# Gathered rows ordered behind the products of each step, and other rates of gathering

## The chip, the cores and the metric

The kernel runs on one core of one Trainium2 chip. The metric is the time of one execution on the device in microseconds (us); less is better. The profile comes from one execution, recorded by the hardware profiler. PE is TensorE (PEld its weight loads), DVE is VectorE, ACT is ScalarE, POOL is GpSimd, SP is SyncE.

## The reference, cut to what matters

Two layers of a transformer trunk run on 256 latent and 256 context tokens of width 1024. Each layer is an adaptive norm, four attention branches, a gated merge, and then an expert layer with a residual. The expert layer is the part that matters here:

```
q = x @ w_q                              # 8 heads, two half queries each
s = q . subkeys ; top 16 of 128 on each half
cand = sums of the two top lists ; best 16 of them -> experts (of 16384), g = softmax(best)
u_sel, v_sel = u[experts], v[experts]    # rows of 1024 floats
a = gelu(x . u_sel)                      # one number for each token, head and choice
y = sum over heads and choices of g * a * v_sel
```

So each token picks 8 x 16 = 128 of 16384 experts; each expert is one row of u and one row of v. The first layer runs this for all 512 tokens, the last layer for the 256 latent tokens alone.

## The kernel before, in words

**Two ways to the same expert layer.** In layer 0, 384 of the 512 tokens take the dense way: all 16384 experts are multiplied (128 blocks of 128 experts), and a matrix G of gate weights, zero for experts that are not chosen, masks the result. The other 128 tokens take the gathered way (class Chosen): for each of the 128 choices, one indirect DMA fetches one row of u for each token, and then, once all dots are known, one row of v for each. That is 256 rows (a "row" here is a tile of 128 tokens x 1024 floats). In layer 1 all 256 tokens are dense.

**The dense stages of layer 0**, in the order of `peer` and `experts`:

- `route` finds the experts. At its end `ahead` runs the first 17 u steps (LEAD0).
- The G stage: u steps 17 to 39 (`u_step`), with 48 g steps between them. A `u_step` loads a block of u, splits it into a high part (ACT, L144) and a low part (L145, on POOL or DVE by a share), and makes 24 products on PE (L183), parked through a Gelu (L753). A `g_step` builds one-hot and gate tiles on DVE (L761, L765, L769) for 8 tokens and multiplies them on PE (L777); the result goes to DRAM. All 48 g steps are asked for by u step 34; the last six u steps follow.
- The mixed steps, 88 of them: `v_step(j)` multiplies a parked block by its gates (L793), splits it and a block of v (L144, L145), and makes 18 products (L804); `u_step(j + 40)` follows it.
- The v steps, the last 40, without a u step.

**The gathered way rides along.** After each u step (G stage) or each v step, `gather()` adds a rate to a counter, and `Chosen.step` runs as many times as the counter holds whole rows. GATHERS holds the rate of the G stage and that of the mixed steps; in the v steps the rate is what is left, divided by 37. One step requests rows until five are under way (AHEAD 4, ROWS 5), and uses the oldest: for u a dot product on DVE (L1085), for v a multiply-add on DVE (L1091). A request is one instruction in POOL's queue (L1062):

```
while self.asked <= min(i + AHEAD, 2 * SLOTS - 1):
    n = self.asked
    self.load()
```

`finish` takes what is left, transposes the result (L1103) and adds it to the residual; `v_end` (L819) does the same for the dense tokens, and the statistics of the next norm follow.

**What sets the order of the work.** Each engine takes its instructions in the order of its own queue. The queues are laid out before the run by a planner that simulates a timeline (`schedule_with_timeline_sim=True`): an instruction is put into its queue when, in the plan, its inputs are there and its engine is free. The program's order ranks what is ready at the same time; it doesn't hold anything back. An explicit edge can: with the kind that is used here (NoSync) an instruction is placed only after another one is placed, and the engines get no semaphore for it. The kernel has one use of such edges, `issue_after` in `route`, between instructions of PE.

Of the kernel before, what the change touches and what calls it, by code (L numbers as in the profile page):

```python
# [55 lines left out]
MB = [2, 3]  # L56
SHARE = [0.64, 0.888, 0.75]
PSH = [[1.0, 0.65, 0.6], [1.0, 0.3, 0.3]]
GATHERS = [1.0, 2.15]
SHL = [0.3, 0.181]  # L60
DIRECT = 7
NST = 16
# [6 lines left out]
class K:  # L69
    def __init__(self, tc, a, out):  # L70
        self.tc, self.nc, self.a, self.out = tc, tc.nc, a, out
        self.n_lo = 0.0
        self.fresh = False
        self.gates = []
        self.rows = None
        self.fill = []
        self.share = 0.5
# [646 lines left out]
    def peer(self):  # L724
# [4 lines left out]
        tc, nc, a, l = self.tc, self.nc, self.a, self.l  # L729
# [3 lines left out]
        lead = LEAD[l]  # L733
        with self.pool("pe") as hp, tc.tile_pool(name="gd", bufs=1, space=bass.MemoryType.DRAM) as dp:
# [9 lines left out]
            P, park, grs, vacc, stage = [], {}, {}, {}, {}  # L744
# [3 lines left out]
            def u_step(j):  # L748
                hi, lo = self.weights(a["u"][l, j])
                ps = self.psum("acc")[:, :n]  # L750
                end = self.mm(ps, hi, lo, lambda kt: P[0][:, kt, :n], lambda kt: P[1][:, kt, :n], DT)
                park[j] = hp.tile([128, n], F32, name="park", tag="park", bufs=lead + 1)
                nc.scalar.activation(park[j], ps, AF.Gelu)  # L753
                return end.ins

            def g_step(t0):
# [32 lines left out]
            def v_step(j):  # L789
                w = park.pop(j)  # L790
                g = grs[j // GI][:, :, j % GI, :]
                w3 = w.rearrange("p (b t) -> p b t", t=GB)
                nc.vector.tensor_mul(w3, w3, g)  # L793
                hi, lo = self.weights(a["v"][l, j])
                whi = vp[0].tile([128, n], F32R, name="whi", tag="whi", bufs=WB)
                wlo = vp[0].tile([128, n], F32R, name="wlo", tag="wlo", bufs=WB)
                self.split(whi, wlo, w, self.lo_engine(n / 1024))
                if j == 0:
                    vacc[0] = [[self.psum("big") for _ in range(2)] for _ in range(nt)]
                for x, y, first, end in ((whi, hi, j == 0, False), (wlo, hi, False, False),  # L800
                                         (whi, lo, False, j == 127)):
                    for t in range(nt):
                        for d in range(2):
                            nc.tensor.matmul(vacc[0][t][d], x[:, t * 128:t * 128 + 128],  # L804
                                             y[:, d * 512:d * 512 + 512], start=first, stop=end)

            def v_end():

# [25 lines left out]
            def phase(i, ns):  # L834

                self.share, self.n_lo = PSH[l][i], 0.0
                if self.chosen:
                    r = GATHERS[i] if i < 2 else (2 * SLOTS - self.chosen.at) / (ns - 3)
                    return lambda: self.chosen.steps(r)
                return lambda: None  # L840

            with self.pool("route") as wk:
                own = None
                if self.chosen:
                    own = wk.tile([128, DT, 128], F32, name="own")
                P[:] = self.norm_mod(wk, hp, NB, LAT if self.last else ALL, 1, n, own)
                self.share = SHARE[2]


                def ahead():  # L850
                    self.share, self.n_lo = PSH[l][0], 0.0
                    return [u_step(j) for j in range(LEAD0[l])][-1]

                self.route(wk, n, *P, own, i1T, i2T, gAB, ahead)
            with self.pool("rows") as p:
                if self.chosen:
                    self.chosen.own = p
                self.experts(l, lead, n, gp, vp, u_step, g_step, g_read, v_step, v_end, phase)
# [169 lines left out]
class Chosen:  # L1028
# [3 lines left out]
    def __init__(self, k, pool):  # L1032
        self.k, self.nc, self.pool = k, k.nc, pool
        self.index = pool.tile([128, SLOTS], I32, name="cx")
        self.g = pool.tile([128, SLOTS], F32, name="cg")
        self.dot = pool.tile([128, SLOTS], F32, name="cd")

        self.h = self.y = pool.tile([128, D], F32, name="ch")
        self.at, self.asked, self.ready, self.due, self.rows = 0, 0, 0, 0.0, []

    def tokens(self, own):

        k, nc = self.k, self.nc
        for i in range(2):
            ps = k.psum("big")
            for j in range(4):
                nc.tensor.transpose(ps[:, j * 128:j * 128 + 128], own[:, i * 4 + j, :], k.ident)
            nc.scalar.activation(self.h[:, i * 512:i * 512 + 512], ps, AF.Copy)
# [7 lines left out]
    def load(self):  # L1056
        nc, i = self.nc, self.asked
        if i == 2 * SLOTS or (i < SLOTS and i >= self.ready):
            return
        self.asked += 1  # L1060
        row = self.own.tile([128, D], F32, name="row", tag="row", bufs=ROWS)
        nc.gpsimd.indirect_dma_start(  # L1062
            out=row, out_offset=None,
            in_=self.k.a["u_rows" if i < SLOTS else "v_rows"],
            in_offset=bass.IndirectOffsetOnAxis(ap=self.index[:, i % SLOTS:i % SLOTS + 1], axis=0))
        self.rows.append(row)

    def step(self):

        nc, i = self.nc, self.at  # L1070
# [3 lines that stand above are left out]
            if n == self.asked:  # L1074
                break
        if not self.rows:
            return
        row = self.rows.pop(0)
        self.at += 1
        s = i % SLOTS  # L1080
        if i == SLOTS:
            nc.scalar.activation(self.dot, self.dot, AF.Gelu)
            nc.vector.tensor_mul(self.g, self.g, self.dot)
        if i < SLOTS:
            nc.vector.scalar_tensor_tensor(row, row, 1.0,  # L1085
                                           self.h, op0=OP.mult, op1=OP.mult,
                                           accum_out=self.dot[:, s:s + 1])
        elif s == 0:
            nc.vector.tensor_scalar(self.y, row, self.g[:, 0:1], None, op0=OP.mult)
        else:  # L1090
            nc.vector.scalar_tensor_tensor(self.y, row, self.g[:, s:s + 1], self.y, op0=OP.mult,  # L1091
                                           op1=OP.add)
# [149 lines left out]
```

## Time and profile before

| what | value |
|---|---|
| time, median of 3 runs | 3394.08 us (3390.36 to 3397.08) |
| the profiled execution: its time | 3400.0 us |
| the profiled execution: its span, first to last instruction | 3397.5 us |
| busy: PE | 3112.5 us (92%) |
| busy: DVE | 2371.5 us (70%) |
| busy: POOL | 1496.1 us (44%) |
| busy: ACT | 1366.0 us (40%) |
| granted PE clock, mean | 0.950 |
| bytes read and written in DRAM | 594.99 MB and 42.99 MB |

The span is cut into stretches by the view of stages: there each engine has its busy time, with the number of its instructions in brackets. "Idle before" in a row of the view by lines is the time the engine stood idle just ahead of these instructions, with what ended it. A granted clock of 1.00 stands for 2.4 GHz, 0.50 for 1.2 GHz, and a mean between them for a stretch that had both.

### The profile page before, as it was taken

How to read it: one execution, taken by the hardware profiler on the slowest of the kernel's cores; microseconds unless marked ns; L12 is line 12 of the kernel's file. 1: busy time of each engine (PE TensorE's matmuls, PEld its weight loads, DVE VectorE, ACT ScalarE, POOL GpSimd, SP SyncE). 2: the span in 40 equal slices, each digit the busy share in tenths (PEclk: the TensorE clock that was granted, in tenths of full speed). 3: DMA queues.
4: the chain of work that ended last, by engine and by line, in shares of the span. 5: the costliest groups of instructions: out<-in, count | busy, mean ns of one | idle time of the engine just before them, and what ended most of it. 6: DMA issues, size and time to landing. Idle time of an engine off the chain costs nothing. (4 is left out here: it accounts for less than half of the span.)

```text
span 3397.5 us, 49459 instructions
## 1 busy us (share of the span) xinstructions
PE 3112.5 (92%) x19063; PEld 2731.2 (80%) x19063; DVE 2371.5 (70%) x4092; ACT 1366.0 (40%) x2166; POOL 1496.1 (44%) x814
## 2 busy tenths in 40 slices
PE   7999999888776798999999998999987889999998
PEld 5867777888666587888899887788987888999987
DVE  5465453799999898989944434445689997666655
ACT  4444443323332233333333333345543454444454
POOL 1211322236656688888844332234435563232221
PEclk9998999899788899999999998899988999999999
DMA  6331333124888988998844333443433569666664
GB/s 245 103 99 50 106 118 110 57 86 149 319 304 304 353 296 299 325 319 296 281 154 143 125 130 116 153 137 106 148 131 120 187 217 308 213 210 212 191 193 136
DMA packets 251292, 641.20 MB, mean 189 GB/s; under 512 B 20017, under 2 KB 107697, under 8 KB 245937
## 3 DMA queue, kind: packets, MB, share of 16 engines
q1 hardware_dynamic: 208432, 461.88, 42.1%
q0 software_dynamic: 36864, 134.23, 11.2%
q10 hardware_dynamic: 5760, 41.95, 3.3%
q8 instruction: 149, 2.44, 0.3%
q14 instruction: 87, 0.70, 0.1%
HBM read 594.99 MB, written 42.99 MB: 188 GB/s over the span
## 5 line engine op out<-in xcount | busy, mean ns | idle before, releaser
L145 POOL TENSOR_TENSOR w_lo<-raw,w_hi 128x1024 fp32r<-128x1024 f32 x387 | 974.8, 2521 | 1336.1 <-ACT w_hi L144 831.2
L144 ACT ACTIVATE w_hi<-raw 128x1024 fp32r<-128x1024 f32 x664 | 702.8, 1060 | 1190.9 <-PE ps_acc L183 437.5
L183 PE MATMUL ps_acc<-hhi,w_hi 128*128 128x256 f32 (+2 forms) x3136 | 997.6, 335 | 56.6 <-ACT w_hi L144 21.0
L183 PE MATMUL ps_acc<-hlo,w_hi 128*128 128x256 f32 (+2 forms) x3136 | 972.4, 328 | 0.3 <-DVE hlo L355 0.3
L183 PEld LDWEIGHTS ps_acc<-hhi,w_hi 128*128 128x128 f32 x3136 | 618.0, 197 | 102.1 <-ACT w_hi L144 26.0
L183 PEld LDWEIGHTS ps_acc<-hlo,w_hi 128*128 128x128 f32 x3136 | 615.5, 197 | 27.6 <-issue 0.9
L183 PE MATMUL ps_acc<-hhi,w_lo 128*128 128x256 f32 (+2 forms) x3136 | 580.8, 326 | 46.7 <-POOL w_lo L145 39.4
L145 DVE TENSOR_TENSOR w_lo<-raw,w_hi 128x1024 fp32r<-128x1024 f32 x277 | 355.7, 1285 | 332.9 <-ACT w_hi L144 210.1
L183 PEld LDWEIGHTS ps_acc<-hhi,w_lo 128*128 128x128 f32 x3136 | 498.1, 194 | 81.1 <-POOL w_lo L145 50.6
L804 PE MATMUL ps_big<-w_lo,whi 128*128 128x512 f32 x1280 | 334.8, 391 | 13.4 <-POOL w_lo L145 10.3
L804 PE MATMUL ps_big<-w_hi,whi 128*128 128x512 f32 x1280 | 338.1, 394 | 9.6 <-ACT w_hi L144 5.7
L804 PE MATMUL ps_big<-w_hi,wlo 128*128 128x512 f32 x1280 | 335.5, 391 | 0.3 <-DVE wlo L145 0.3
L793 DVE TENSOR_TENSOR park<-park,gr 128x384 f32<-128x384 f32 (+1 forms) x256 | 234.1, 944 | 131.9 <-ACT park L753 104.8
L145 DVE TENSOR_TENSOR wlo<-park,whi 128x256 fp32r<-128x256 f32 (+1 forms) x214 | 221.1, 1035 | 113.5 <-ACT whi L144 113.4
L804 PEld LDWEIGHTS ps_big<-w_lo,whi 128*128 128x128 f32 x1280 | 238.1, 188 | 67.4 <-POOL w_lo L145 15.0
L804 PEld LDWEIGHTS ps_big<-w_hi,wlo 128*128 128x128 f32 x1280 | 240.6, 188 | 52.7 <-DVE wlo L145 1.0
L804 PEld LDWEIGHTS ps_big<-w_hi,whi 128*128 128x128 f32 x1280 | 235.1, 189 | 51.7 <-ACT w_hi L144 7.1
L1091 DVE SCALAR_TENSOR_TENSOR ch<-row,cg,ch 128x1024 f32<-128x1024 f32 x127 | 241.9, 1905 | 8.3 <-DMA row<-in_v_rows,cx 6.5
L1062 POOL DMA_INDIRECT row<-in_u_rows,cx x128 | 190.7, 1490 | 119.5 <-DVE row L1085 92.2
L1085 DVE SCALAR_TENSOR_TENSOR row<-row,ch 128x1024 f32<-128x1024 f32 x128 | 201.7, 1591 | 16.2 <-DMA row<-in_u_rows,cx 16.2
L1062 POOL DMA_INDIRECT row<-in_v_rows,cx x128 | 179.1, 1399 | 47.7 <-DVE ch L1091 19.6
L777 PE MATMUL ps_big<-p,pg 128*128 128x128 f16 x1280 | 109.7, 250 | 89.8 <-DVE pg L765 46.4
(223 smaller groups left out, 3469.1 us busy)
## 6 DMA issues: line engine op xcount, KB each, us to landing
raw<-in_u SPq DMA_DIRECT2D x256, 512.0 KB
raw<-in_v SPq DMA_DIRECT2D x256, 512.0 KB
raw<-in_w_mod SPq DMA_DIRECT2D x96, 512.0 KB
G<-stage ACTq DMA_DIRECT2D x40, 1024.0 KB
raw<-in_w_gate SPq DMA_DIRECT2D x64, 512.0 KB
gr<-G SPq DMA_DIRECT2D x16, 1536.0 KB
raw<-in_w_in SPq DMA_DIRECT2D x40, 512.0 KB
raw<-in_w_q SPq DMA_DIRECT2D x32, 512.0 KB
```

The costliest lines, as they stand in the source:

```text
L144: nc.scalar.activation(hi, src, AF.Copy)
L145: (lo_engine or nc.vector).tensor_sub(lo, src, hi.bitcast(F32))
L183: end = nc.tensor.matmul(ps, w[:, kt * 128:kt * 128 + 128], x(kt), start=i == 0, stop=i == 3 * nk - 1)
L777: nc.tensor.matmul(ps[:, t], pg[:, z, :, b + t], p1[:, b + t, :], start=z == 0, stop=z == 1)
L793: nc.vector.tensor_mul(w3, w3, g)
L804: nc.tensor.matmul(vacc[0][t][d], x[:, t * 128:t * 128 + 128], y[:, d * 512:d * 512 + 512], start=first, stop=end)
L1062: nc.gpsimd.indirect_dma_start(out=row, out_offset=None, in_=self.k.a["u_rows" if i < SLOTS else "v_rows"], in_offset=bass.IndirectOffsetO ...
L1085: nc.vector.scalar_tensor_tensor(row, row, 1.0, self.h, op0=OP.mult, op1=OP.mult, accum_out=self.dot[:, s:s + 1])
L1091: nc.vector.scalar_tensor_tensor(self.y, row, self.g[:, s:s + 1], self.y, op0=OP.mult, op1=OP.add)
```

## The change

Two new rates: 0.3 rows for each u step of the G stage where it was 1.0, and 2.35 for each mixed step where it was 2.15. `Chosen` gets a field `behind`, which holds the last product of the last u step, and in the v steps that of the last v step. Each request gets an edge of the order-only kind to that product.

```diff
-GATHERS = [1.0, 2.15]
+GATHERS = [0.3, 2.35]
...
                 nc.scalar.activation(park[j], ps, AF.Gelu)
+                if self.chosen:
+                    self.chosen.behind = end.ins
                 return end.ins
...
                     for t in range(nt):
                         for d in range(2):
-                            nc.tensor.matmul(vacc[0][t][d], x[:, t * 128:t * 128 + 128],
-                                             y[:, d * 512:d * 512 + 512], start=first, stop=end)
+                            m = nc.tensor.matmul(vacc[0][t][d], x[:, t * 128:t * 128 + 128],
+                                                 y[:, d * 512:d * 512 + 512], start=first, stop=end)
+                if self.chosen and j + lead >= 128:
+                    self.chosen.behind = m.ins
...
         self.at, self.asked, self.ready, self.due, self.rows = 0, 0, 0, 0.0, []
+        self.behind = None
...
-        nc.gpsimd.indirect_dma_start(
+        dma = nc.gpsimd.indirect_dma_start(
             out=row, out_offset=None,
...
         self.rows.append(row)
+        if self.behind:
+
+            self.k.tc.add_manual_dep(dma.ins, self.behind.name, mybir.DependencyInfo(
+                mybir.DependencyClass.NoSync, mybir.DependencyReason.DATA), reason="pace")
```

## Rows read from the trace of the kernel before

**Rows 1.** The page: DVE's busy share in 40 slices of 85 us, in tenths.

```profile
DVE  5465453799999898989944434445689997666655
```

**Rows 2.** The view of stages: stretch, its length, busy us (instructions), clock, DMA share, GB/s.

```profile
835.00:1095.00 260.00, 183.13 (x1494) 168.81 (x1494) 260.00 (x289) 83.70 (x138) 159.53 (x92) 0.81 0.88 312
1095.00:1130.00 35.00, 19.51 (x145) 16.63 (x143) 16.46 (x28) 5.85 (x8) 22.88 (x15) 0.74 0.98 346
1130.00:1200.00 70.00, 59.16 (x275) 50.51 (x276) 68.43 (x93) 21.72 (x31) 47.04 (x25) 0.96 1.07 342
1200.00:1690.00 490.00, 458.86 (x2252) 406.21 (x2251) 443.54 (x317) 165.02 (x215) 416.31 (x240) 0.99 0.89 306
1280.00:1320.00 40.00, 33.83 (x161) 29.93 (x160) 28.50 (x30) 12.53 (x17) 29.29 (x19) 0.96 0.93 313
1690.00:1915.00 225.00, 225.00 (x1139) 204.75 (x1138) 102.13 (x75) 84.74 (x108) 83.82 (x39) 1.00 0.44 142
1915.00:2080.00 165.00, 165.00 (x732) 136.84 (x732) 60.02 (x46) 61.56 (x78) 63.95 (x32) 1.00 0.35 115
2640.00:2810.00 170.00, 143.32 (x1353) 139.32 (x1353) 164.61 (x95) 81.83 (x135) 106.44 (x36) 0.96 0.60 205
```

**Rows 3.** By lines, 835 to 1095 (count, busy us, mean ns, idle before).

```profile
L1062 POOL DMA_INDIRECT row<-in_u_rows,cx x72 | 108.4, 1506 | 90.0 <-DVE row L1085 74.4 <-PE ps_big L777 9.8 <-issue 3.8
L1085 DVE SCALAR_TENSOR_TENSOR row<-row,ch 128x1024 f32<-128x1024 f32 x70 | 102.7, 1473 | 0.0
...
L777 PE MATMUL ps_big<-p,pg 128*128 128x128 f16 x752 | 68.0, 260 | 63.2 <-DVE pg L765 42.4 <-DVE p L769 20.7
...
L145 POOL TENSOR_TENSOR w_lo<-raw,w_hi 128x1024 fp32r<-128x1024 f32 x20 | 52.1, 2604 | 9.6 <-ACT w_hi L144 7.6 <-issue 1.7
```

**Rows 4.** By tile `row`, whole span: min/median/max ns, first and last start.

```profile
L1062 POOL DMA_INDIRECT row<-in_u_rows,cx x128: 937/1682/1990, 830.5 to 1283.1; - x128
...
L1062 POOL DMA_INDIRECT row<-in_v_rows,cx x128: 937/1300/2496, 1287.4 to 1677.7; - x128
L1091 DVE SCALAR_TENSOR_TENSOR ch<-row,cg,ch x127: 1270/1285/7229, 1298.9 to 1692.1; 128x1024 f32<-128x1024 f32 x127
```

**Rows 5.** Timeline of DVE from 862 us: start, duration.

```profile
862.21 1.21 DVE L765 TENSOR_TENSOR pg<-p,gAB 128x2048 f16<-128x2048 f16 x1
863.35 1.21 DVE L1085 SCALAR_TENSOR_TENSOR row<-row,ch 128x1024 f32<-128x1024 f32 x1
...
864.49 1.22 DVE L1085 SCALAR_TENSOR_TENSOR row<-row,ch 128x1024 f32<-128x1024 f32 x1
```

**Rows 6.** By lines, 1200 to 1690: the rows' work on DVE and POOL.

```profile
L1091 DVE SCALAR_TENSOR_TENSOR ch<-row,cg,ch 128x1024 f32<-128x1024 f32 x125 | 239.4, 1915 | 8.2 <-DMA row<-in_v_rows,cx 6.5
...
L1062 POOL DMA_INDIRECT row<-in_v_rows,cx x128 | 179.1, 1399 | 47.7 <-DVE ch L1091 19.6 <-issue 18.6 <-DVE w_lo L145 2.4
...
L1085 DVE SCALAR_TENSOR_TENSOR row<-row,ch 128x1024 f32<-128x1024 f32 x31 | 60.4, 1969 | 7.4 <-DMA row<-in_u_rows,cx 7.4
```

**Rows 7.** Waits, 1200 to 1690: PE for low parts from POOL (total, times, longest).

```profile
PE ps_acc L183 <- POOL w_lo L145: 12.8, 14, 2.0
PE ps_big L804 <- POOL w_lo L145: 10.3, 9, 2.6
```

**Rows 8.** Timeline from 1448 us: one multiply-add on DVE, and POOL's last subtraction beside it.

```profile
1448.53 6.89 DVE L1091 SCALAR_TENSOR_TENSOR ch<-row,cg,ch 128x1024 f32<-128x1024 f32 x1 [0.23 <-DMA row<-in_v_rows,cx]
...
1451.96 2.38 POOL L145 TENSOR_TENSOR w_lo<-raw,w_hi 128x1024 fp32r<-128x1024 f32 x1
```

**Rows 9.** By lines, 1925 to 2075 (v steps alone): the subtractions.

```profile
L145 POOL TENSOR_TENSOR w_lo<-raw,w_hi 128x1024 fp32r<-128x1024 f32 x21 | 50.4, 2400 | 83.7 <-PE ps_big L804 68.3 <-ACT w_hi L144 15.3
L145 DVE TENSOR_TENSOR wlo<-park,whi 128x384 fp32r<-128x384 f32 x27 | 38.2, 1416 | 50.0 <-ACT whi L144 50.0
L145 DVE TENSOR_TENSOR w_lo<-raw,w_hi 128x1024 fp32r<-128x1024 f32 x16 | 19.6, 1225 | 46.8 <-PE ps_big L804 27.8 <-ACT w_hi L144 19.1
L145 POOL TENSOR_TENSOR wlo<-park,whi 128x384 fp32r<-128x384 f32 x8 | 8.2, 1026 | 0.0
```

## The prediction

> **What bounds the kernel now.** I read the page first. Over the whole span PE is busy for 92% (the table above), but DVE's slices show a run of nines in the middle [rows 1], where the gathered rows are worked on. So I cut layer 0's expert layer into stretches [rows 2] and ask of each which engine is full. There are four.
>
> - G stage, 835 to 1095: DVE is busy for all of its 260.0 us, PE for 183.1 at a granted clock of 0.81, between the levels of 1.2 and 2.4 GHz [rows 2]. PE's products of the g steps stood idle for 63.2 us, ended by the gate tiles of DVE [rows 3]. DVE is the bound.
> - The last u steps of that stage and the change of pools, 1095 to 1130: PE busy for 19.5 of 35 us [rows 2].
> - Mixed steps, 1130 to 1915. From 1690 on, when no rows are left (the last multiply-add starts at 1692.1 [rows 4]), PE is busy for 225.0 of 225 us [rows 2]. That is the speed PE alone allows. The 40 v steps from 1915 to 2080 fill 165.0 of 165 us, 4.12 us each. A mixed step has 24 products more; 27 of the 88 steps lie in the 225 us, so it takes 8.33 us.
> - From 1200 to 1690, with rows, PE is busy for 458.9 of 490 us [rows 2]: 458.9/8.33 = 55.1 steps, and 31.1 us lost. The view of waits puts 12.8 and 10.3 us of that on low parts that POOL delivers late [rows 7].
>
> The rows themselves are the last thing to see. The program asks for one dot for each u step of the G stage, so 23 dots and 27 requests by its end. The trace has 72 requests and 70 dots by 1095 [rows 3], and the requests of u start at 830.5 [rows 4]. The planner put them wherever POOL and DVE had room in its plan; the program's order held nothing back. On the chip DVE has no room there.
>
> **G stage: dots that leave a full engine.** With the edge, a request can be placed only behind the products of its u step. The counter gets 0.3 for each of the 17 or 18 u steps beside the g steps: 5 dots, and 4 rows more under way. So 65 of 70 dots leave the stretch. What does one cost? Its mean is 1.473 us [rows 3], but that holds waiting which would pass to the next instruction. Start to start, a dot takes 1.14 us, as does a gate tile (862.21, 863.35, 864.49 [rows 5]). So DVE's need falls by 65 x 1.14 = 74 us, to 186. Layer 1 has the same stage with no rows in it: there DVE is busy for 164.6 of 170 us, 97% [rows 2]. 186/0.97 = 192, so 68 us go. PE must fit too: 183.1 us at clock 0.81 would be about 148 at full clock (an estimate from that row), under 192. From above, 65 x 1.473 = 96 us. From below, if PE's clock stays and PE reaches no more than layer 1's 143.3/170 = 84%, the stage takes 183/0.843 = 217 and gives back 43. I take -68, which rests on the nearest stage without rows.
>
> POOL gains too: its requests stood for 74.4 us behind a dot that had to free a row [rows 3], with the splits of u queued behind them. I book nothing for it, because PE waited for DVE then.
>
> **1095 to 1130.** From 1200 on the trace has 125 multiply-adds and 31 dots [rows 6], so of the 256 rows about 30 fall between 1095 and 1200. Those before 1130 leave. DVE was busy for under half of this piece, PE lost 15.5 us at clock 0.74 [rows 2]. I take -6, with bounds 0 and -15.5. The 10.8 us lost from 1130 to 1200 I leave: rows stay there.
>
> **Mixed steps.** Before, 156 rows [rows 6] in 55.1 steps: 2.83 each, and 31.1/156 = 0.20 us of PE lost for each row. After, 6 rows are done before, and 88 steps take 207, 2.35 each. Load for each step: DVE 443.5/55.1 = 8.05 us, less 0.48 rows of 1.915 us [rows 6], gives 7.13 or 86% of 8.33 (it was 90.5% of the 490 us). POOL 416.3/55.1 = 7.56, less 0.48 x 1.399 [rows 6], gives 6.89 or 83% (85%). So it is the same coupling, with somewhat more slack, over more rows. At 45% of DVE nothing was lost (1690 to 1915). I take half the price, 0.10 us for a row: 21 us for 31, so -10. Bounds: nothing lost, -31; the old price, 41 for 31, +10.
>
> **V steps.** Here rows are new: 256 - 6 - 207 = 43. DVE goes from 60.0 to 60.0 + 43 x 1.915 = 142 of 165 us, 86%; POOL from 64.0 to 64.0 + 43 x 1.399 = 124, 75%. DVE is loaded as in the mixed steps before, POOL less. At the old price, 0.20 for a row, +9. Bounds: 0, and every row on PE's path at its bare 1.27 us (the least of [rows 4]), +55. What DVE does there now hides behind 4.12 us of products; that is the cover that could run out.
>
> **The wait that is added.** The edge gives POOL no semaphore; it sets the place in POOL's queue. Behind a request stand the splits of u and v, which PE waits for (23 us before [rows 7]). Two or three requests for each step, 1.4 us each, now come together behind a u step's products, where they were spread. That is in the price of a row, and a rival below. SP's queue of weight loads is passed by nothing. DMA carries the same bytes: about 0.9 of its time with rows before, 0.44 and 0.35 without [rows 2]; spreading 43 rows of 524 KB over 165 us adds 137 GB/s to 115, under the 312 of the G stage.
>
> **The end.** Rows must be done before the last transposes. The rate ends three v steps early, 12 us, against one dot; and at 2080 these transposes stand in the queue today. I book 0, at most +5.
>
> **Sum.** -68 - 6 - 10 + 9 = -75. The profiled execution took 3400.0 us (span 3397.5), so 3325. It lay 5.9 us over the median of 3394.08, so the median should be 3319. The likeliest case alone spans 3300 to 3345.
>
> **Rivals.**
>
> *B, more comes back.* The mixed steps run at PE's speed with fewer rows in each, the v steps hide theirs. -74 - 12 - 31 + 0 = -117: 3277. For it: PE's waits for POOL make up only 23 of the 31 us lost, with POOL's load lower now [rows 7]. Against: DVE at 86%.
>
> *C, DVE and POOL exclude each other.* A multiply-add that takes 1.27 us at its least lasted 6.89 from 1448.53, and ended 1.08 us after POOL's last subtraction did, 1451.96 + 2.38 = 1454.34 [rows 8]. So POOL's subtractions count against DVE. In 36.4 v steps (150 us) POOL's took 58.6 us and DVE's, at their 0.55 (its share of 1.22 for the full tile) and 1.22 us bare, 34 [rows 9]: 2.55 us for a step. With 1.16 rows at 1.27 it is 4.02, just under 4.12. With rows at 1.915 it is 4.77, over it by 0.65: 40 x 0.65 = +26. With the old price in the mixed steps, +10: -68 - 6 + 10 + 26 = -38, 3356. For it: the long multiply-add. Against: 1.915 already holds some of POOL's time, counted twice here. The Trainium skill, page "SBUF — State Buffer", section "Who interferes with whom", states the rule behind this: an instruction of DVE with two inputs in SBUF and one of GpSimd that reads SBUF share a port as an exclusive lock, and the later one blocks fully. By that rule the change carries dots from a stage where POOL subtracts for 52 of 260 us to one where it does so for 58.6 of 150, which speaks against it; the trace agrees that DVE waits (5.6 us of the 6.89 in that one instruction).
>
> *D, slower: requests in front of splits.* Bunched requests hold up POOL's splits at each of the 128 steps. The price is that of the worst stretch so far: 1280 to 1320, PE busy for 33.83 of 40 us [rows 2], a factor of 1.18. Then 88 x 8.33 x 1.18 + 165 x 1.18 = 1060 us, against 950 from 1130 to 2080: +110, less 74: +36, 3430. It decides from a factor of 1.14. For it: PE's waits for POOL. Against: that stretch is the worst of its stage, whose mean factor is 490/458.9 = 1.07, and POOL's load falls.
>
> *E, the edge does nothing.* Between engines no wait in the trace shows such an edge at work. If the planner doesn't hold to it, requests float up as before and the rates change nothing: 3394.
>
> **How the numbers follow.** A 0.57, B 0.17, C 0.13, D 0.07, E 0.06. The three faster cases make 0.87. E is within 0.2% (7 us, about what can be told from no change) but for 0.01, so same 0.05; slower 0.08. The range runs from B less a little, 3270, to 3385, where the weak G stage (+25) meets the old price in the mixed steps (+20) and a v stage at half of its bound (+18), and a little over. It leaves out D, E and a twentieth of the rest.
>
> **What would show it.** Right: about 5 dots in the G stage, DVE still full there, the stage at 185 to 200 us instead of 260, PE's idle time behind gate tiles down; requests of v lasting to within 20 us of the last v step; PE at 95% or more in the mixed steps and some per cent idle in the v steps. Wrong: 70 dots in the G stage (E); v steps over 4.8 us (C, D); PE's waits for POOL's low parts well over 23 us (D).

## The result and the profile after

The changed kernel takes 3295.22 us (median of 4 runs, 3292.48 to 3316.38) against 3393.26 for the kernel before, run beside it: a ratio of 0.9724, 95% interval 0.9683 to 0.9765. The profiled execution took 3292.5 us with a span of 3290.7; the one of before had 3400.0 and 3397.5, so 107 us lie between the two traces. The forecast was 3319.

The view of stages of the changed kernel, cut where its stages end (first and last product of the g steps, first product of a v step, last parked u step, first transpose of `finish`). Columns as in [rows 2]: stretch, length, PE, PEld, DVE, ACT, POOL busy, clock, DMA share, GB/s.

```profile
833.90:1026.50 192.60, 158.56 (x1462) 145.55 (x1462) 174.00 (x167) 79.08 (x136) 78.23 (x28) 0.91 0.65 237
1026.50:1051.80 25.30, 13.77 (x130) 11.82 (x127) 10.91 (x22) 7.01 (x12) 4.88 (x3) 0.81 1.05 330
1051.80:1809.20 757.40, 740.78 (x3698) 670.66 (x3699) 616.41 (x568) 274.77 (x354) 611.52 (x343) 0.99 0.87 295
1809.20:1975.40 166.20, 163.91 (x720) 134.68 (x719) 132.93 (x89) 60.45 (x77) 127.15 (x70) 1.00 0.70 241
```

The kernel before, cut at the same events:

```profile
838.40:1097.90 259.50, 182.63 (x1494) 168.59 (x1494) 259.50 (x291) 83.96 (x140) 158.80 (x92) 0.81 0.87 309
1097.90:1131.20 33.30, 16.65 (x122) 13.93 (x120) 14.76 (x24) 5.77 (x9) 20.83 (x14) 0.71 1.03 360
1131.20:1916.90 785.70, 744.88 (x3673) 663.33 (x3674) 612.90 (x481) 271.93 (x354) 547.17 (x303) 0.99 0.78 262
1916.90:2080.00 163.10, 163.10 (x722) 134.94 (x721) 60.02 (x46) 60.50 (x77) 63.95 (x32) 1.00 0.35 113
```

| stretch | before | after | difference | forecast |
|---|---|---|---|---|
| G stage | 259.5 | 192.6 | -66.9 | -68 |
| last u steps, change of pools | 33.3 | 25.3 | -8.0 | -6 |
| 88 mixed steps | 785.7 | 757.4 | -28.3 | -10 |
| 40 v steps | 163.1 | 166.2 | +3.1 | +9 |
| sum | 1241.6 | 1141.5 | -100.1 | -75 |

The other 7 us lie outside: 4.5 ahead of the first g step and 2.2 behind the last v step. Among the experiments that leave the splits ahead of the g steps as they were, the first g step lies between 834 and 842, so I read nothing into them.

Where the rows went shows in the view by tile `row` (min/median/max ns, first and last start), to be held against [rows 4]: the last request and the last multiply-add, which started at 1678 and 1692, now start at 1944 and 1953, with the first transpose behind the v products at 1975.

```profile
L1067 POOL DMA_INDIRECT row<-in_u_rows,cx x128: 937/1302/1977, 844.9 to 1489.8; - x128
...
L1067 POOL DMA_INDIRECT row<-in_v_rows,cx x128: 937/1296/2962, 1496.4 to 1943.7; - x128
L1100 DVE SCALAR_TENSOR_TENSOR ch<-row,cg,ch x127: 1269/1285/7265, 1506.5 to 1953.4; 128x1024 f32<-128x1024 f32 x127
```

In the G stage 9 dots are left of 72, and PE's idle time ahead of the products of the g steps fell from 63.2 us [rows 3] to 17.9. DVE now stands idle for 18.6 us of the stage, 17.2 of it ahead of gate tiles, ended by PE. The view by lines from 835 to 1020, and in the second fence DVE's gate tiles from 833.9 to 1026.5:

```profile
L145 POOL TENSOR_TENSOR w_lo<-raw,w_hi 128x1024 fp32r<-128x1024 f32 x17 | 61.0, 3593 | 107.9 <-ACT w_hi L144 100.4 <-issue 7.5
...
L779 PE MATMUL ps_big<-p,pg 128*128 128x128 f16 x715 | 57.8, 241 | 17.9 <-DVE p L771 9.1 <-DVE pg L767 8.7
...
L1067 POOL DMA_INDIRECT row<-in_u_rows,cx x9 | 13.8, 1532 | 2.0 <-issue 1.2 <-ACT stage L782 0.3 <-DVE modT L306 0.2
L1094 DVE SCALAR_TENSOR_TENSOR row<-row,ch 128x1024 f32<-128x1024 f32 x9 | 12.1, 1346 | 1.3 <-DMA row<-in_u_rows,cx 1.3
```

```profile
L767 DVE TENSOR_TENSOR pg<-p,gAB 128x2048 f16<-128x2048 f16 x47 | 65.1, 1387 | 17.2 <-PE ps_big L779 17.2
```

In the mixed steps PE's waits for low parts from POOL, 23.1 us in 490 [rows 7], are gone. These are all PE's waits on the other engines from 1051 to 1809 by the view of waits (total, times, longest); the 10.8 is the start of the first v step:

```profile
PE ps_big L806 <- ACT w_hi L144: 16.5, 4, 10.8
PE ps_acc L183 <- ACT w_hi L144: 7.8, 2, 4.6
PE ps_acc L183 <- DVE w_lo L145: 2.9, 2, 1.4
PE ps_acc L183 <- POOL w_lo L145: 0.2, 1, 0.2
```

### The profile page after: what moved, and what is told of

Read it like the earlier page. It is cut to its first block, busy times and chain, and to the rows that moved or that the text cites. A ratio compares the mean times of both kernels' runs of the same rounds, so it can differ in the third digit from the quotient of the medians.

```text
span 3290.7 us, 49451 instructions
## 1 busy us (share of the span) xinstructions
PE 3074.5 (93%) x19063; PEld 2707.9 (82%) x19063; DVE 2361.8 (72%) x4092; ACT 1366.5 (42%) x2166; POOL 1527.7 (46%) x814
## 5 line engine op out<-in xcount | busy, mean ns | idle before, releaser
L145 POOL TENSOR_TENSOR w_lo<-raw,w_hi 128x1024 fp32r<-128x1024 f32 x387 | 1008.7, 2611 | 1306.8 <-ACT w_hi L144 959.4
L183 PEld LDWEIGHTS ps_acc<-hhi,w_hi 128*128 128x128 f32 x3136 | 611.4, 195 | 94.4 <-ACT park L753 21.2
L183 PEld LDWEIGHTS ps_acc<-hlo,w_hi 128*128 128x128 f32 x3136 | 608.8, 194 | 27.8 <-DVE hlo L355 1.5
L806 PE MATMUL ps_big<-w_hi,whi 128*128 128x512 f32 x1280 | 341.6, 394 | 17.2 <-ACT w_hi L144 17.2
L1100 DVE SCALAR_TENSOR_TENSOR ch<-row,cg,ch 128x1024 f32<-128x1024 f32 x127 | 232.3, 1829 | 68.7 <-DMA row<-in_v_rows,cx 67.6
L1094 DVE SCALAR_TENSOR_TENSOR row<-row,ch 128x1024 f32<-128x1024 f32 x128 | 211.8, 1670 | 77.2 <-DMA row<-in_u_rows,cx 76.7
L145 DVE TENSOR_TENSOR wlo<-park,whi 128x256 fp32r<-128x256 f32 (+1 forms) x214 | 203.0, 951 | 48.0 <-ACT whi L144 47.9
L1067 POOL DMA_INDIRECT row<-in_u_rows,cx x128 | 181.6, 1419 | 34.0 <-issue 18.3
L753 ACT ACTIVATE park<-ps_acc 128x384 f32<-128x384 f32 (+1 forms) x256 | 110.6, 432 | 120.5 <-PE ps_acc L183 117.9
```

The source lines that it names most:

```text
L145: (lo_engine or nc.vector).tensor_sub(lo, src, hi.bitcast(F32))
L183: end = nc.tensor.matmul(ps, w[:, kt * 128:kt * 128 + 128], x(kt), start=i == 0, stop=i == 3 * nk - 1)
L806: m = nc.tensor.matmul(vacc[0][t][d], x[:, t * 128:t * 128 + 128], y[:, d * 512:d * 512 + 512], start=first, stop=end)
L1067: dma = nc.gpsimd.indirect_dma_start(out=row, out_offset=None, in_=self.k.a["u_rows" if i < SLOTS else "v_rows"], in_offset=bass.IndirectO ...
L1094: nc.vector.scalar_tensor_tensor(row, row, 1.0, self.h, op0=OP.mult, op1=OP.mult, accum_out=self.dot[:, s:s + 1])
```

## The experiments

Ratios are to the kernel before, of runs on the same chip, with 95% intervals. Stretches are from one profiled execution each, cut as above; that execution can lie some us from the median (15 over it in experiment 4, 12 under it in experiment 6), so a difference of a few us between two stretches isn't clear of noise.

**1. The rates alone, without the edge.**

```diff
# kernel before
-GATHERS = [1.0, 2.15]
+GATHERS = [0.3, 2.35]
```

> The new rates without the edge. Theory 1 (the planner puts a request wherever its plan has room, only the edge holds it back): as the kernel before, 3393 us within 10, some 70 dots in the G stage (835 to 1095). Theory 2 (the rates in the program's order do it, the edge is idle): as the changed kernel, 3295, with under 15 dots in the G stage.

3393.74 us, ratio 0.9992 (0.9978 to 1.0005): nothing. The G stage has 72 requests as before (by tile, in that stretch):

```profile
L1062 POOL DMA_INDIRECT row<-in_u_rows,cx x72: 1002/1682/1987, 835.9 to 1095.5; - x72
L1085 DVE SCALAR_TENSOR_TENSOR row<-row,ch x72: 1210/1212/3783, 836.5 to 1095.5; 128x1024 f32<-128x1024 f32 x72
```

Theory 1 holds: without the edge the rate in the program's text doesn't reach the queue.

**2. The edge alone, with the old rates.**

```diff
# changed kernel
-GATHERS = [0.3, 2.35]
+GATHERS = [1.0, 2.15]
```

> The edge with the old rates 1.0 and 2.15. Theory 1 (each dot in the G stage costs the 1.14 us of DVE that it takes): 17 to 23 dots in the G stage where the changed kernel has 9 to 11, so about 12 more, +14 us; 189 rows in the mixed steps instead of 207, which run at PE's speed either way; about 3308 us. Theory 2 (the rates do it): 3393. Theory 3 (the G stage is not bound by DVE once requests are paced): 3295.

3302.95 us, ratio 0.9731 (0.9695 to 0.9767); the changed kernel's interval overlaps it almost whole. G stage and mixed steps by the view of stages:

```profile
839.40:1041.10 201.70, 159.51 (x1459) 147.46 (x1459) 200.19 (x192) 81.61 (x137) 90.36 (x40) 0.89 0.72 259
...
1069.20:1818.90 749.70, 739.46 (x3698) 670.86 (x3699) 570.55 (x533) 275.17 (x354) 577.30 (x325) 0.99 0.85 286
```

22 dots stand in the G stage, DVE is full again (200.2 of 201.7), and it is 9.1 us longer than with 9 dots. The number is that of the program: 18 u steps with one row each, and the 4 more that are under way. The mixed steps, with 2.15 rows each, are 7.7 us shorter. So the edge makes the gain, and the two new rates shift a few us between stages, too little to tell apart in the medians.

**3. Short dots: DVE's share of the rows taken away.**

```diff
# kernel before
-            nc.vector.scalar_tensor_tensor(row, row, 1.0,
-                                           self.h, op0=OP.mult, op1=OP.mult,
+            nc.vector.scalar_tensor_tensor(row[:, :64], row[:, :64], 1.0,
+                                           self.h[:, :64], op0=OP.mult, op1=OP.mult,
```

> The kernel before, but each dot runs over 64 of the 1024 numbers (that part of the computation is left out); requests, their bytes and the 128 multiply-adds stay. Theory 1 (DVE's time for dots bounds the G stage): the 70 dots shrink from 1.2 to under 0.2 us, the G stage falls from 260 to some 190 us although as many requests or more stand in it, and the whole to about 3310 to 3325. Theory 4 (the requests slow the G stage, by their bytes at a DMA share of 0.88 or by POOL's time): the G stage stays over 240 us and the whole over 3375.

3348.09 us, ratio 0.9854 (0.9828 to 0.9880). With 60 requests still in it and DMA busier than before, the G stage fell from 259.5 to 200.5; but the piece after it grew from 33.3 to 46.2, and the mixed steps stayed at 788.0:

```profile
840.90:1041.40 200.50, 153.44 (x1422) 140.07 (x1422) 177.21 (x265) 75.11 (x131) 121.38 (x78) 0.92 0.94 350
1041.40:1087.60 46.20, 21.77 (x169) 19.14 (x166) 14.21 (x41) 10.68 (x17) 20.27 (x16) 0.83 1.06 383
1087.60:1875.60 788.00, 749.75 (x3697) 669.81 (x3698) 549.56 (x488) 274.70 (x354) 538.77 (x315) 0.99 0.78 267
```

For the G stage theory 1 holds. The whole missed its forecast (3310 to 3325) by 23 us or more: the G stage gave back 10 us less than forecast, and the piece after it grew by 13; why it grew was not tested.

**4. Short requests: the bytes taken away.**

```diff
# kernel before
-        row = self.own.tile([128, D], F32, name="row", tag="row", bufs=ROWS)
+        row = self.own.tile([128, 64], F32, name="row", tag="row", bufs=ROWS)
...
-            in_=self.k.a["u_rows" if i < SLOTS else "v_rows"],
+            in_=self.k.a["u_rows" if i < SLOTS else "v_rows"].rearrange("n (a b) -> (n a) b", b=64),
...
+        wide = row[:, None, :].to_broadcast([128, 16, 64])
...
```

> The kernel before, but each request fetches 64 numbers of a row instead of 1024 (the rest is left out of the computation); DVE's dots and multiply-adds still run over 1024 elements, by reading the 64 again. Theory 1 (DVE bounds the G stage): as many dots in the G stage as there are, each 1.14 us; with 60 or more of them the stage stays at 240 us or over and the whole within 25 us of 3393. Theory 4 (bytes of the requests slow the stages): DMA share in the G stage falls from 0.88 to about 0.5, and the whole to about 3300.

3402.85 us, ratio 1.0024 (1.0011 to 1.0036): with a sixteenth of the bytes nothing is won.

```profile
838.90:1069.60 230.70, 167.53 (x1488) 154.24 (x1487) 230.70 (x238) 83.26 (x138) 127.13 (x68) 0.86 0.53 192
...
1095.60:1936.80 841.20, 763.80 (x3697) 674.52 (x3698) 630.84 (x517) 274.66 (x354) 563.85 (x329) 0.98 0.46 145
```

The planner now put 46 dots into the G stage, DVE was full, and the stage took 230.7. It is 28.8 us shorter with 26 dots fewer: at 1.14 us each the dots account for 29.6, so nothing is left for the bytes. The mixed steps took 841 at a DMA share of 0.46; more rows were packed into their first part (up to 35 requests in 80 us, against 20 to 28 in the kernel before), which fits the loss but was not tested by itself. The bytes are not what costs; theory 4 falls, for both stages.

**5. More rows for each mixed step, with the edge.**

```diff
# changed kernel
-GATHERS = [0.3, 2.35]
+GATHERS = [0.3, 2.9]
```

> The changed kernel with 2.9 rows for each mixed step instead of 2.35, so all 250 remaining rows fall into 86 mixed steps, 28 in 80 us (the kernel before had 24 to 28 there and lost 6% of PE, the changed one has 21 to 24 and loses 1%). Theory M1 (the rate of rows sets PE's loss in the mixed steps, with or without the edge): the mixed steps take about 785 to 790 us instead of 757, the v steps 163 instead of 166, the whole about 3320 to 3330. Theory M2 (where the edge places the requests does it, whatever the rate): the mixed steps stay under 765 us, the whole at 3288 to 3298.

3336.37 us, ratio 0.9816 (0.9793 to 0.9840). The mixed steps took 807.5 us instead of 757.4, the v steps 163.1; the waits on POOL's low parts are back:

```profile
PE ps_big L806 <- ACT w_hi L144: 26.1, 7, 11.2
PE ps_acc L183 <- POOL w_lo L145: 16.5, 15, 2.7
PE ps_acc L183 <- DVE w_lo L145: 10.5, 6, 2.7
```

M1 holds and M2 falls: the edge has no virtue in the mixed steps beyond the rate that it enforces. It came out worse than forecast (785 to 790): a step took 0.85 us over the 8.33 of PE alone, where the 55 steps with rows of the kernel before took 0.56 over it at nearly the same rate. What makes this difference was not tested.

**6. More rows left for the v steps.**

```diff
# changed kernel
-GATHERS = [0.3, 2.35]
+GATHERS = [0.3, 1.6]
```

> The changed kernel with 1.6 rows for each mixed step, so about 109 rows are left for 37 v steps, 2.95 each. Theory C (POOL's subtractions and DVE's two-input work exclude each other): 2.55 us for a v step and 2.95 x 1.27 = 3.75 for its rows make 6.3 us against 4.12 of products, so the v stage takes 166 + 80 = about 245 us and the whole about 3365. Theory of the old price (0.2 us for a row): v stage about 180, mixed steps 750, the whole about 3300.

3367.83 us, ratio 0.9926 (0.9907 to 0.9946). The v stage took 257.0 us, near theory C's 245, but in another form than I had drawn: its products ended some 57 us before the rows did. The wait of the transposes for the last multiply-add says it (timeline):

```profile
2055.70 1.97 PE L1112 MATMUL ps_acc<-ident,ch 128*128 128x128 f32 x8 [57.49 <-DVE ch L1100]
```

So rows that are too many for the v steps lengthen them, to about 200 us here, and the rest falls behind the end.

**7. Less in the mixed steps, a bit more in the v steps.**

```diff
# changed kernel
-GATHERS = [0.3, 2.35]
+GATHERS = [0.3, 2.15]
```

> The changed kernel with the old rate of 2.15 in the mixed steps and the new 0.3 in the G stage; 61 rows are left for the v steps, 1.65 each. If the mixed steps gain as in the kernel with the edge alone (750 us against 757) and the v steps still hide their rows (166): 3288. If the v steps are at the end of their cover with 43 rows (theory C: 2.55 + 1.65 x 1.27 = 4.65 us against 4.12): v stage 186 us, the whole about 3308.

3303.38 us, ratio 0.9731 (0.9714 to 0.9748). Mixed steps 751.8, v steps 181.9: with 61 rows for the v steps their cover is gone (theory C: 186), with 43 it was not (166.2).

**8. No rows in the G stage.**

```diff
# changed kernel
-GATHERS = [0.3, 2.35]
+GATHERS = [0.0, 2.45]
```

> The changed kernel with no rows in the G stage and 2.45 for each mixed step. Theory 1 (each dot in the G stage takes 1.14 us of a full DVE): nine dots fewer, -10 us, 3285. Theory 5 (with nine dots DVE is no longer full, 174 of 192.6 us busy, and PE's chain sets the stage): 0 to -3 in the G stage, and the mixed steps, with 215 rows, lose up to 5 more: 3292 to 3300.

3296.42 us, ratio 0.9704 (0.9686 to 0.9721): about as the changed kernel. Inside, neither theory had it: the G stage gave back more than either said (15.4 us), and the mixed steps lost as much (20.6). DVE's busy time in the G stage hardly fell, from 174.0 to 172.5 us; what went is its idle time, so these 15.4 us are not the time of nine dots on a full DVE. And half of the loss in the mixed steps is one wait: from 1490 on PE stands for 9.8 us, for a high part whose block of u came late; its load stood in SP's queue behind one that waited 8.9 us for DVE.

```profile
839.20:1016.40 177.20, 150.78 (x1463) 140.68 (x1462) 172.52 (x149) 78.99 (x136) 70.61 (x19) 0.95 0.65 235
1016.40:1039.60 23.20, 13.40 (x129) 11.74 (x127) 8.50 (x20) 6.81 (x12) 3.68 (x2) 0.88 0.99 304
1039.60:1817.60 778.00, 748.05 (x3697) 673.81 (x3698) 648.49 (x588) 274.13 (x353) 630.53 (x355) 0.98 0.87 295
```

**9 and 10. A lower share of the subtractions for POOL**, with 2.35 and with 2.9 rows for each mixed step.

```diff
# changed kernel (9); the same with GATHERS = [0.3, 2.9] (10)
-PSH = [[1.0, 0.65, 0.6], [1.0, 0.3, 0.3]]
+PSH = [[1.0, 0.3, 0.3], [1.0, 0.3, 0.3]]
```

> The changed kernel with POOL's share of the subtractions lowered to 0.3 in the mixed steps (from 0.65) and in the v steps (from 0.6); DVE takes the rest. Theory C (DVE and POOL exclude each other in these subtractions, so one on POOL costs the pair 2.4 us and one on DVE 1.14): the pair's need falls by about 0.9 us for each mixed step and 0.4 for each v step; mixed steps 757 to 745 or less, v stage 166 to 164, the whole about 3280. Rival (DVE's own load is what PE waits for): DVE gets 0.9 us more for each mixed step, 9.0 with the waiting that it has now against 8.33, and the whole goes to 3320 or more.

> The same lower share with 2.9 rows for each mixed step, to be set against the kernel with 2.9 rows and the old share (mixed steps 807.5 us, whole 3336). Theory C: bare need of the pair for each mixed step falls from 8.5 to 7.5 us against 8.33 of products, so the mixed steps come back to 750 to 765 and the whole to about 3285. Rival (DVE's own load): mixed steps over 830 us, the whole over 3355.

9: 3284.83 us, ratio 0.9672 (0.9649 to 0.9695; this overlaps the changed kernel's interval); mixed steps 748.4, v steps 163.0. 10: 3300.38 us, ratio 0.9720 (0.9700 to 0.9739), 15 us over its forecast; mixed steps 756.3, where the old share took 807.5. A row's instruction got shorter on DVE though DVE had more to do: with 2.9 rows and the old share (first fence, kernel of experiment 5), and with the lower share (second):

```profile
L1100 DVE SCALAR_TENSOR_TENSOR ch<-row,cg,ch 128x1024 f32<-128x1024 f32 x127 | 221.6, 1745 | 37.5 <-DMA row<-in_v_rows,cx 35.8
L1094 DVE SCALAR_TENSOR_TENSOR row<-row,ch 128x1024 f32<-128x1024 f32 x118 | 193.0, 1657 | 32.4 <-DMA row<-in_u_rows,cx 32.2
```

```profile
L1100 DVE SCALAR_TENSOR_TENSOR ch<-row,cg,ch 128x1024 f32<-128x1024 f32 x127 | 193.8, 1526 | 23.0 <-DMA row<-in_v_rows,cx 22.0
...
L1094 DVE SCALAR_TENSOR_TENSOR row<-row,ch 128x1024 f32<-128x1024 f32 x118 | 152.3, 1313 | 5.2 <-DMA row<-in_u_rows,cx 5.2
```

Theory C holds, and the rival of DVE's own load falls in both. The starts and durations in the two traces show what made DVE's instructions shorter. Both kernels have 245 dots and multiply-adds in the mixed steps. With the old share 87 of them ran beside one of POOL's subtractions, with the lower share 47. Those that met none took 1.25 us on average and never more than 1.33, in both kernels, though most ran beside a request of POOL. So POOL's subtractions hold DVE up, and its requests don't. POOL's queue also got shorter; how much of PE's gain comes from that, these two runs don't separate.

**11 and 12. The two combined: no rows in the G stage, and POOL's share lowered**, in 12 in the G stage too.

```diff
# changed kernel (11); in 12 the first list is [0.3, 0.3, 0.3]
-PSH = [[1.0, 0.65, 0.6], [1.0, 0.3, 0.3]]
-GATHERS = [0.3, 2.35]
+PSH = [[1.0, 0.3, 0.3], [1.0, 0.3, 0.3]]
+GATHERS = [0.0, 2.45]
```

> POOL's share at 0.3 in mixed and v steps, no rows in the G stage, 2.45 for each mixed step. Without rows the G stage and the piece after it took 200.4 us instead of 217.9, but at the old share the mixed steps lost 20.6 of that. Theory C: at the lower share the mixed steps stay at 750 to 755 with 2.45 rows, so the 17 us are kept: about 3270. If the mixed steps lose them again (over 765): 3285.

> The same with POOL's share lowered in the G stage too, from 1.0 to 0.3. Theory C: 17 subtractions there cost the pair about 2 us each on POOL and 1.14 on DVE, so some 12 of them moved give back up to 10 us if DVE still sets the stage: about 3262. If PE's chain sets it (DVE 172 of 177 us busy without rows speaks against): 3270; if the planner puts the subtractions behind gate tiles that the g steps wait for: over 3275.

11: 3264.06 us, ratio 0.9617 (0.9596 to 0.9638). 12: 3262.49, ratio 0.9616 (0.9599 to 0.9632). Both beat the changed kernel (0.9724), and can't be told apart. The stages of 11:

```profile
838.80:1014.00 175.20, 148.92 (x1462) 137.85 (x1462) 173.67 (x148) 79.70 (x136) 68.68 (x19) 0.96 0.66 238
1014.00:1047.40 33.40, 14.56 (x128) 12.91 (x126) 8.67 (x20) 6.65 (x12) 8.12 (x7) 0.76 0.91 286
1047.40:1793.50 746.10, 737.67 (x3697) 669.00 (x3698) 589.77 (x662) 275.00 (x353) 432.95 (x276) 0.99 0.87 304
1793.50:1956.60 163.10, 163.10 (x721) 134.98 (x721) 120.11 (x105) 60.53 (x77) 85.77 (x53) 1.00 0.69 242
```

With 2.45 rows the mixed steps take 746.1 where the old share took 778.0. In 12 the G stage shrank by another 10.5 us, to 164.7, as theory C said (up to 10), but the medians don't show it: the first g step came 7.4 us later, at 846.2 instead of 838.8, since the lower share also holds for the 17 u steps ahead of the stage, so most of the gain was paid before it.

## Why the prediction was right, and where its sizes were off

**The direction and the mechanism.** The step that carried the forecast was that rows leave a stage in which DVE is full. Three kernels have a full DVE there and different numbers of full dots: 72 dots 259.5 us, 46 dots 230.7 (short requests), 22 dots 201.7. That is 57.8/50 = 1.16 us for each dot, next to the start-to-start time of 1.14 [rows 5] that the sum used. Below that DVE is no longer full: 9 dots 192.6, none 177.2, which is 0.70 and 1.71 us for each dot that left.

That the term came out at -66.9 for -68 is luck in part. The sum had DVE busy for 186 us and idle for 6; the trace has 174.0 and 18.6. DVE's busy time fell by 85.5 us for 63 dots, 1.36 each: part of the waiting in their mean of 1.473 left with them, which I had thought would pass to the next instruction. Against it, DVE now waits for PE. These two errors of 12 us cancelled. I had also counted 5 dots where there were 9: only a request has the edge, so the 4 rows that were under way got their dots in the stage too. PE's clock rose from 0.81 to 0.91, so the weak bound (PE's clock stays, 43 us back) was far off.

**Where the whole landed.** 3295 lies under the span of the likeliest case (3300 to 3345), a little nearer to rival B's 3277 than to the forecast of 3319. What moved it there is the mixed steps, below.

**That the edge is at work** (rival E): shown. Experiment 1 has the rates and not the edge, and nothing happens; experiment 2 has the edge and not the rates, and nearly all of it happens. That the new rates themselves are worth next to nothing was not in the forecast.

**The mixed steps, the term that was mis-sized:** -10 forecast, -28.3 measured, close to its outer bound of -31. PE's idle time there fell from 40.8 us to 16.6. About 10 of it lie in the first 70 us in both kernels, as forecast; behind them 31.1 fell to 6.3, where I had priced 21, half of the old 0.20 us for a row, as if the loss were spread evenly over rows. (The other 4 us came off PE's busy time.) The prediction's own loads said more than I read in them: I set DVE's 86% of 8.33 us against 90.5% of the 490 us; against 8.33 us too, the old load was 97%.

The runs look like a limit instead. With POOL's share as it was, the mixed steps took 744.8 us at 1.6 rows for each, 749.7 and 751.8 at 2.15, 757.4 at 2.35, 778.0 at 2.45 and 807.5 at 2.9 (experiments 6, 2, 7, the changed kernel, 8, 5; one profile each, and 9.8 us of the 778.0 are the single wait of experiment 8). Up to 2.35 PE hides nearly all; 0.55 more cost 50. Add up the bare need of DVE and POOL as if they never ran at once. The counts for a step are these rows of the kernel before, 1200 to 1690, divided by 53:

```profile
L145 POOL TENSOR_TENSOR w_lo<-raw,w_hi 128x1024 fp32r<-128x1024 f32 x72 | 180.7, 2512 | 13.8 <-ACT w_hi L144 12.3 <-issue 0.3
...
L793 DVE TENSOR_TENSOR park<-park,gr 128x384 f32<-128x384 f32 x53 | 61.4, 1159 | 13.3 <-ACT park L753 13.3
...
L145 DVE TENSOR_TENSOR w_lo<-raw,w_hi 128x1024 fp32r<-128x1024 f32 x35 | 53.8, 1538 | 16.7 <-ACT w_hi L144 13.2 <-issue 2.7 <-PE ps_big L804 0.8
L145 DVE TENSOR_TENSOR wlo<-park,whi 128x384 fp32r<-128x384 f32 x40 | 43.9, 1097 | 0.9 <-ACT whi L144 0.8
...
L145 POOL TENSOR_TENSOR wlo<-park,whi 128x384 fp32r<-128x384 f32 x13 | 16.7, 1285 | 0.1
```

Their means hold waiting; the bare times are start to start on DVE (from 1455.35, 1456.49, 1456.96 and 1458.15 in the timeline of the kernel before: a full tile 1.14 us, a small one or a gate 0.48, a multiply-add 1.2) and the shortest on POOL (2.4 and 1.0). A step then has on DVE 0.48 us for its gates, 0.75 x 0.48 and 0.66 x 1.14 for subtractions, and on POOL 1.36 x 2.4 and 0.25 x 1.0 of them: 5.1 us, and 1.2 for each row. That is 7.9 at 2.35 rows, 8.0 at 2.45 and 8.6 at 2.9, against PE's 8.33. So the loss begins a little under the limit, and is large over it. A sum of this kind stood in rival C for the v steps; I had not made it for the mixed ones, and it would have moved the forecast most of the way to B.

**The v steps:** +3.1 for +9. Rival C's own price for them, +26, used a row's time with waiting in it (1.915 us); its other reading, 4.02 us against 4.12 with bare times, was the right one: 43 rows just fit. (The 0.55 in that sum is not the share of 1.22 that it is called, which would be 0.46; the sum would then be 3.96.) At 61 rows they don't (181.9), at 109 still less (257.0 with the tail).

**Rival C** was wrong as a forecast of this change (3356) and right as a mechanism: experiments 7, 9 and 10 came out near its arithmetic, and the traces show the exclusion itself. In the mixed steps of the kernel before, 99 of the 174 dots and multiply-adds met no subtraction of POOL, and none of them took over 1.29 us; the 75 that met one took 2.71 us on average. The Trainium skill's page "SBUF — State Buffer", section "Who interferes with whom", gives the rule; the runs agree with its consequence, that moving a subtraction from POOL (2.4 us) to a busy DVE (1.14 us bare) relieves DVE's rows. That the later one blocks, as the prediction cites the rule, is not what its long multiply-add shows: it started at 1448.53 [rows 8] and stood through three subtractions of POOL, each begun after it. The first two are

```profile
1448.67 2.37 POOL L145 TENSOR_TENSOR w_lo<-raw,w_hi 128x1024 fp32r<-128x1024 f32 x1
...
1451.00 1.01 POOL L145 TENSOR_TENSOR wlo<-park,whi 128x384 fp32r<-128x384 f32 x1
```

**Rival D** (requests in front of POOL's splits): PE's waits for POOL in the mixed steps went from 23.1 us to 0.2 at this rate, so it fell; at 2.9 rows they came back, with the rate.

**The piece after the G stage** came out at -8.0 for -6. The end cost nothing, as booked: the last multiply-add started 22 us before the first transpose. One sign missed: requests were to last to within 20 us of the last v step, and the last one started 32 us before the first transpose.

## What to carry to other kernels

Where a planner lays out the queues, a rate that stands only in the program's order may not reach the chip: look in the trace at when the side work ran, and pace it with an edge to the main engine's work. Then find the rate by the stage: add the bare times of engines that exclude each other and hold the sum some way under the main engine's time for a step. Here the loss was small up to 7.9 us of 8.33 and large at 8.6, and not in proportion to the rows. And when side work crowds an engine, look whether the helper that was meant to relieve it costs it more than it saves.

## What the runs showed of the hardware that was not expected

The exclusion works both ways. With fewer dots around them, POOL's subtractions in the G stage took longer, not shorter: a mean of 3593 ns for 17 in the changed kernel (835 to 1020) against 2604 for 20 before [rows 3]. One of them lasted 5.87 us while DVE made one-hot and gate tiles back to back, and ended 2.2 us after the last of these did, about the 2.4 us that it takes alone:

```profile
1010.04 5.87 POOL L145 TENSOR_TENSOR w_lo<-raw,w_hi 128x1024 fp32r<-128x1024 f32 x1 [23.28 <-ACT w_hi L144]
...
1010.76 1.21 DVE L767 TENSOR_TENSOR pg<-p,gAB 128x2048 f16<-128x2048 f16 x1
...
1011.89 1.21 DVE L771 TENSOR_TENSOR p<-iota,i1T 128x1024 f16<-128x1024 f16 x1
...
1013.03 0.68 DVE L763 TENSOR_TENSOR p<-iotaT,i2T 128x1024 f16<-128x1024 f16 x1
```

PE waited 7.8 us for such subtractions in that stretch. In both long cases the engine that waited was not served when the other ended one instruction: here POOL waited through three tiles of the g steps begun after it, there the multiply-add of [rows 8] through three subtractions.

POOL's requests took longer beside such work too. In the kernel before, from 838 to 1917, the 12 that had little work of DVE with two inputs beside them took 0.94 to 0.96 us, the 210 that ran almost wholly beside it 0.94 to 2.01, with a median of 1.63. DVE was not held in turn: beside a request alone, no dot or multiply-add of the mixed steps took over 1.29.

DVE's idle time for rows to land rose as well, from 16.2 and 6.5 us over the whole kernel before (dots and multiply-adds) to 77.0 and 67.6. PE's idle time in the mixed steps fell all the same.
